# Exponent rows of a state-space layer: spread over partitions by one-hot matmuls, or by transfers from DRAM

## The chip, the cores and the metric

The kernel runs on one core of a Trainium2 chip. A core has TensorE for matmuls (PE in the profile, with its weight loads as PEld), VectorE (DVE), ScalarE (ACT), GpSimd (POOL) and SyncE (SP), each with a queue of its own that is worked off in order, and 16 DMA engines that all queues share. The metric is the time of one execution in device microseconds; the median of three runs before the change is 2631.59 us.

## The reference, cut to what matters

A two-layer encoder on 528 positions (16 meta tokens and 512 tokens) of 2048 channels, in float32. The change touches only the first layer's Mamba-2 branch, which has 32 heads in 8 groups of 4 and runs in both directions. The positions form 6 chunks of 88 in the kernel. For each head and direction, with `A_cs` the running sum of `log_a` inside a chunk:

```
seg    = A_cs[:, :, :, None] - A_cs[:, :, None, :]
Lmat   = exp(where(tri, seg, -inf))
CB     = einsum("bclgn,bcsgn->bclsg", Cc, Bc)
Y_diag = einsum("bclsgr,bcsgrp->bclgrp", CB[..., None] * Lmat, X)
Xd     = X * exp(A_cs[:, :, -1:] - A_cs)[..., None]
states = einsum("bclgn,bclgrp->bcgrpn", Bc, Xd)
...
Y_off  = einsum("bclgn,bcgrpn->bclgrp", Cc, prev) * exp(A_cs)[..., None]
y      = Y_diag + Y_off
```

Around it stand an input projection (97 weight panels of 128 columns, one of them half as wide), a 31-tap depthwise convolution on other channels, output projections, and a second layer with neighbourhood attention.

## The kernel before, in words

Channels lie on partitions and the 528 positions along the free axis. `proj` takes one panel of weights: two halves of 8 blocks, each weight split into a high and a low part (`wh` by ACT at L261, `wl` by DVE at L264), and for every block three products times two column halves of 264, so 96 matmuls into one PSUM tile `ps` (L308). There are two `ps` buffers, three of `raw` (the panel half as loaded by SP, L157), three of `wh` and of `wl`.

The layer's input projection runs over the groups `g` = 0 to 7. Each group takes one or two pairs of gated-convolution panels (`glu_tile`: gate `sg` L659 to L661, value `up` L666) and then six panels: `bT`, `cT`, two `xs` (each evacuated by DVE at L434 and convolved, L437 to L440) and two `zt` (evacuated by DVE at L685, SiLU at L686). After each panel `step()` lets two queues of background generators emit work up to a budget: `bgs` (budget `SB_` = 7000), which holds `ssd(g)`, and `bgc` (budget 6000), which holds `conv31` (31 taps on DVE, L452, ending in a store to `cv_d`, L455). `ssd(g)` is queued at the end of group g, so that it is emitted during the panels of group g+1. Each `yield` in it gives the budget that it has used; once a `step()` has used up its budget, the rest waits for the next panel.

`ssd(g)` does the following. It forms `pc`, the product of B and C (L555); for six chunks it transposes (L568), scales (L573) and multiplies out the states `st` (L578); then four steps of the recurrence over chunks on `pv` (L587, L590). Then come two halves `i` = 0, 1 of two heads `j` each. For each head it needs the row of running sums `fc` of that head, both directions, on every partition:

- `pf` = that row on all 128 partitions: two matmuls per direction with a one-hot column `sel` as stationary operand and `fhl` (the 64 rows of `fc` as a high and a low part) as moving one (L603);
- `T` (88 partitions): ReLU of `pf` against a column bias, chunk by chunk, 12 instructions of 88 by 88 on ACT (L606), Exp (L609), 12 scalings on ACT (L616), masks and sum on DVE (L617, L619);
- `cq` (128 partitions): Exp of `pf` on ACT (L608), times C on DVE (L610, L611).

With both heads done, 64 matmuls make `py` (L638); DVE adds and gates it (L642, L643), POOL stores it to `yz_d` (L644), and its square is added up using the `zt` tile as scratch (L648, L649). `T` and `cq` have two buffers each, so a half's tiles come free when the `py` of the half before is done. `pc`, `pf` and `py` share one PSUM buffer, the tag `big`. `zt` has two buffers: the two of the group being worked off by `ssd`, each free when its half is done.

The order of instructions on each engine is not the order of emission. A planner at build time (`schedule_with_timeline_sim=True`) simulates the program with its own costs and puts each engine's instructions into the order in which it sees them become ready, earlier emission first. On the chip that order is then fixed.

Of the kernel before, what the change touches and what calls it, by code (L numbers as in the profile page):

```python
# [12 lines left out]
F32 = mybir.dt.float32  # L13
F32R = mybir.dt.float32r
AF = mybir.ActivationFunctionType
ALU = mybir.AluOpType

P = 128
# [6 lines left out]
L = NM + S  # L25
HL = L // 2
# [4 lines left out]
HPG = 4  # L31
HD = 64
CH = 88
NC = L // CH
NH = 32
# [18 lines left out]
SB_, CB_ = 7000, 6000  # L54
# [29 lines left out]
def hybrid_encoder(ctx: ExitStack, tc: tile.TileContext, hT, win, wdt, wout, oin, oout, par, con,  # L84
                   rpb, out, dbg=None):
    nc = tc.nc
    dbg = dbg or {}

    cp = ctx.enter_context(tc.tile_pool(name="cp", bufs=1))
# [3 lines left out]
    dr = ctx.enter_context(tc.tile_pool(name="dr", bufs=1, space=bass.MemoryType.DRAM))  # L93
# [8 lines left out]
    def pool(**kw):  # L102
        return tc.tile_pool(reuse_waits="tile", **kw)

    def pr(n, a=0, b=None):
        lo, hi = PAR[n]
        return prm[:, lo + a:(hi if b is None else lo + b)]

    def cn(n):
        lo, hi = CON[n]  # L110
        return cst[:, lo:hi]
# [4 lines left out]
    def h2(ap):  # L116
        return ap.rearrange("p (a b) -> p a b", a=2)
# [2 lines left out]
        return h2(ap)[:, :, NB:]  # L120

    yz_d = dr.tile([KT, P, L], F32, name="yz_d")
    cv_d = dr.tile([KT, P, L], F32, name="cv_d")
    pt_d = dr.tile([KT, P, L], F32, name="pt_d")
    yb_d = dr.tile([KT, P, L], F32, name="yb_d")
# [29 lines left out]
    def load(a, hf, pool=None, tag="raw", bufs=3):  # L155
        raw = (pool or wp).tile([P, KH, a.shape[2]], F32, name=tag, tag=tag, bufs=bufs)
        nc.sync.dma_start(raw, a[:, hf * KH:(hf + 1) * KH, :])  # L157
        return raw
# [220 lines left out]
    with ExitStack() as c0:  # L379
        psb = c0.enter_context(tc.tile_pool(name="psb", bufs=1, space=bass.MemoryType.PSUM))  # L380
        sp = c0.enter_context(tc.tile_pool(name="sp", bufs=1))
        dp = c0.enter_context(tc.tile_pool(name="dp", bufs=1))
# [4 lines left out]
        nc.scalar.activation(rs0[:, 0:1], rs0[:, 0:1], AF.Sqrt)  # L387
        first_x = sp.tile([P, 2, L], F32, name="hraw", tag="T", bufs=2)
        wd0 = load(wdt, 0)
# [5 lines left out]
        fetch()()  # L395
        for tag, n, bufs in (("T", 2, 2), ("T", 2, 2), ("cq", 2, 2), ("cq", 2, 2), ("xb", 4, 1), ("pv", 4, 1)):
            t = first_x if not raws else sp.tile([P, n, L], F32, name="hraw", tag=tag, bufs=bufs)
            for i in range(n):
                k = len(raws)
# [17 lines left out]
                if k >= 2:  # L417
                    nc.vector.tensor_tensor(ac, ac, raw, op=ALU.add)

        sel = cp.tile([P, 64], F32R, name="sel")  # L420
        nc.vector.tensor_copy(sel, cn("sel"))
        xp = [sp.tile([P, L + 4], F32, name=f"xp{i}") for i in range(2)]
        for t in xp:
            nc.gpsimd.memset(t[:, 0:2], 0.0)
# [2 lines left out]
        J = 64  # L427
# [62 lines left out]

        t4 = [sp.tile([P, 2, L], F32, name=f"dt{i}", tag=tg, bufs=2) for i, tg in enumerate(("T", "T", "cq", "cq"))]
        v, e, w, z, la, fc, wd, dexp = [t4[i // 2][:J, i % 2] for i in range(8)]
# [25 lines left out]
        nc.gpsimd.memset(rf[:, ::CH], 0.0)  # L518
        nc.vector.tensor_tensor_scan(fc[0:32], rf[0:32], la[0:32], 0.0, ALU.mult, ALU.add)
        nc.vector.tensor_tensor_scan(fc[32:64, ::-1], rf[32:64], la[32:64, ::-1], 0.0, ALU.mult, ALU.add)  # L520
        fhl = dp.tile([P, L], F32R, name="fhl")
        nc.scalar.activation(fhl[:J], fc, AF.Copy)
        nc.vector.tensor_tensor(fhl[J:], fc, fhl[:J].bitcast(F32), op=ALU.subtract)
        fc3 = fc.rearrange("p (c t) -> p c t", c=NC)
        wd3 = wd.rearrange("p (c t) -> p c t", c=NC)
        nc.vector.tensor_tensor(wd3[0:32], fc3[0:32, :, CH - 1:CH].to_broadcast([32, NC, CH]), fc3[0:32], op=ALU.subtract)
# [14 lines left out]
        for nm, src in (("fcol", fc), ("dcol", dt), ("wcol", wd)):  # L541
# [3 lines left out]
            t = dp.tile([CH, NC, 2, NH], F32, name=nm)  # L545
            nc.vector.tensor_copy(t.rearrange("p c r h -> p (c r h)"), pt[:CH, :NC * J])
            cols.append(t)
        fcol, dcol, wcol = cols

        def ssd(g, bT, cT, xs, zs):  # L550
            xb = sp.tile([CH, NC, 3 * P], F32, name="xb", tag="xb")
            pv = sp.tile([P, NC - 1, 2, 256], F32, name="pv", tag="pv")
            pc = psb.tile([P, 2, 512], F32, name="pc", tag="big")
# [11 lines left out]
            for c in range(NC):  # L565
                pt = psb.tile([P, 512], F32, name="pt", tag="sm", bufs=2)
                for i, src in enumerate((xs[0], xs[1], bT)):
# [11 lines left out]
                                 start=True, stop=True)  # L579
# [12 lines left out]
            for i in range(2):  # L592
                gs, cs = [], []
                for j in range(2):
                    hl = 2 * i + j
                    hd = HPG * g + hl
                    T = sp.tile([CH, 2, L], F32, name="T", tag="T", bufs=2)
                    cq = sp.tile([P, 2, L], F32, name="cq", tag="cq", bufs=2)
                    for d in range(2):
                        pf = psb.tile([P, 2, 512], F32, name="pf", tag="big")  # L600
                        jj = d * NH + hd
                        for n in range(2):
                            nc.tensor.matmul(pf[:, n, :HL], sel[:, jj:jj + 1].to_broadcast([P, P]),  # L603
                                             fhl[:, n * HL:(n + 1) * HL], start=True, stop=True)
                        for c in range(NC):
                            nc.scalar.activation(T[:, d, c * CH:(c + 1) * CH], pf[:CH, c // 3, (c % 3) * CH:(c % 3 + 1) * CH],  # L606
                                                 AF.Relu, bias=fcol[:, c, d, hd:hd + 1], scale=-1.0)
                        nc.scalar.activation(h2(cq[:, d]), pf[:, :, :HL], AF.Exp)  # L608
                    nc.scalar.activation(T, T, AF.Exp, scale=-1.0)  # L609
                    nc.vector.tensor_tensor(cq[:, 0, CH:], cq[:, 0, CH:], cT[:, CH:], op=ALU.mult)  # L610
                    nc.vector.tensor_tensor(cq[:, 1, :L - CH], cq[:, 1, :L - CH], cT[:, :L - CH], op=ALU.mult)  # L611
                    yield 1050
                    for d in range(2):
                        for c in range(NC):
                            sl = slice(c * CH, (c + 1) * CH)
                            nc.scalar.activation(T[:, d, sl], T[:, d, sl], AF.Copy, scale=dcol[:, c, d, hd:hd + 1])  # L616
                        nc.vector.tensor_tensor(T[:, d], T[:, d], cbs[d], op=ALU.mult)  # L617
                    yield 1900
                    nc.vector.tensor_tensor(T[:, 0], T[:, 0], T[:, 1], op=ALU.add)  # L619
                    yield 650  # L620
                    gs.append(T)
                    cs.append(cq)
                py = psb.tile([P, 2, 512], F32, name="py", tag="big")
                for c in range(NC):
                    sl = slice(c * CH, (c + 1) * CH)
                    terms = [[], []]
                    for j in range(2):
                        hs = slice((2 * i + j) * HD, (2 * i + j + 1) * HD)
                        terms[j].append((xb[:, c, hs], gs[j][:, 0, sl]))
                        if c > 0:  # L630
                            terms[j].append((pv[:, c - 1, 0, hs], cs[j][:, 0, sl]))
                        if c < NC - 1:
                            terms[j].append((pv[:, NC - 2 - c, 1, hs], cs[j][:, 1, sl]))
                    nt = len(terms[0])
                    for q in range(nt):
                        for j in range(2):
                            a, b = terms[j][q]
                            nc.tensor.matmul(py[j * HD:(j + 1) * HD, c // 3, (c % 3) * CH:(c % 3 + 1) * CH], a, b,  # L638
                                             start=(q == 0), stop=(q == nt - 1))
                ti = 2 * g + i  # L640
                y = xs[i]
                nc.vector.scalar_tensor_tensor(h2(y), h2(y), pr("dd", ti, ti + 1), py[:, :, :HL], op0=ALU.mult, op1=ALU.add)  # L642
                nc.vector.tensor_tensor(y, y, zs[i], op=ALU.mult)  # L643
                nc.gpsimd.dma_start(yz_d[ti], y)  # L644
                if ti == 0:
                    nc.scalar.activation(accy, y, AF.Square)
                else:
                    nc.scalar.activation(zs[i], y, AF.Square)  # L648
                    nc.vector.tensor_tensor(accy, accy, zs[i], op=ALU.add)  # L649
                yield 2100  # L650

        def step():
            pump(bgs, SB_)
            pump(bgc, CB_)
# [56 lines left out]
    with ExitStack() as c1:  # L711
        psb = c1.enter_context(pool(name="psc", bufs=1, space=bass.MemoryType.PSUM))
        zb = c1.enter_context(pool(name="zbp", bufs=14))
        big = c1.enter_context(pool(name="big", bufs=16))
# [33 lines left out]
        for m in range(KT):  # L748
            ps = proj(us, ls)
            t = zb.tile([P, L], F32, name="zb", tag="zb")  # L750
# [301 lines left out]
    with ExitStack() as c2:  # L1052
        psb = c2.enter_context(pool(name="psd", bufs=1, space=bass.MemoryType.PSUM))
        ak = c2.enter_context(pool(name="ak", bufs=1))
        ap = c2.enter_context(pool(name="ap", bufs=1))
# [181 lines left out]
        with tc.manual_schedule(engines={eng.PE, eng.DVE, eng.Activation, eng.Pool}):  # L1237
# [6 lines left out]
            g = filler()  # L1244
# [72 lines left out]
    with ExitStack() as c3:  # L1317
        psr = c3.enter_context(pool(name="pr", bufs=1, space=bass.MemoryType.PSUM))
        op = c3.enter_context(pool(name="op", bufs=NRES))
# [60 lines left out]
        for m in range(2 * NORMF):  # L1380
# [7 lines left out]
            t = op.tile([P, S], F32, name="fo", tag="o")  # L1388
# [221 lines left out]
```

## Time and profile before

| | |
|---|---|
| median of the runs | 2631.59 us (2630.65 to 2633.07) |
| profiled execution: time, span | 2635.39 us, 2633.6 us |
| granted TensorE clock | 0.996 |
| PE, PEld, DVE, ACT, POOL busy over the span | 99%, 94%, 78%, 54%, 14% |
| first matmul `pf` to last | 148.9 to 1046.0 us |
| `pf` matmuls (L603) | 128 |
| Exp of `pf` into `cq` (L608) | 64, 40.0 us in all |
| GpSimd's DMA queue | 78.30 MB, 11.1% of the 16 engines |

The span is divided among the first layer's input projection, which holds everything that the change touches and ends at about 1290 us, and later stages that it leaves alone. A line of the profile gives a line of the kernel, the engine, the operation, output and inputs by name, and times; "x6" means six instructions; what follows "<-" is what released a wait. The profiled execution's time is 3.8 us above the median of the runs.

### The profile page before, as it was taken

What the parts mean: (1) busy time and instruction counts of PE and PEld (TensorE: products, weight loads), DVE (VectorE), ACT (ScalarE), POOL (GpSimd) and SP (SyncE); (2) the same over time, 40 slices, a digit from 0 to 9 for tenths busy, and PEclk for the clock granted to TensorE, in tenths of its full rate; (3) what the DMA queues carried; (4) which work ended last, traced back from release to release, by engine and by line L of the source; (5) the groups of instructions that cost most, each with busy time, mean ns of one, the idle gap of its engine ahead of it and who ended that gap; (6) DMA issues with size and microseconds to landing.
All of it is one profiled execution on the core that took longest, in us unless ns stands there. A gap on an engine that the chain in (4) does not pass through costs nothing.

```text
span 2633.6 us, 52716 instructions
## 1 busy us (share of the span) xinstructions
PE 2599.0 (99%) x21236; PEld 2484.8 (94%) x21236; DVE 2051.0 (78%) x3046; ACT 1419.4 (54%) x2652; POOL 367.5 (14%) x588
## 2 busy tenths in 40 slices
PE   8999999999999999999999999999999999999997
PEld 8999999999999999999999999999999987777797
DVE  6985967887686969997688888877777776666876
ACT  5366585666658566325554556644334355556543
POOL 0000000000000001100220312300000052442133
PEclk9999999999999999999999999999999999999998
DMA  4322223222222222533875877755555454543754
GB/s 173 99 75 93 81 77 97 82 94 74 92 85 76 88 90 92 177 109 111 268 232 166 297 216 236 238 159 163 154 152 159 142 155 124 134 128 116 244 171 152
DMA packets 163173, 373.28 MB, mean 142 GB/s; under 512 B 40896, under 2 KB 70784, under 8 KB 162928
## 3 DMA queue, kind: packets, MB, share of 16 engines
q1 hardware_dynamic: 137840, 289.96, 34.5%
q0 software_dynamic: 23072, 78.30, 11.1%
q8 instruction: 167, 2.74, 0.4%
q10 hardware_dynamic: 2016, 1.65, 0.2%
q14 instruction: 78, 0.64, 0.1%
HBM read 320.59 MB, written 49.25 MB: 140 GB/s over the span
## 4 chain that ended last, share of the span: by engine, by line
PE 88%; DVE 4%; ACT 3%; DMA 3%; issue 1%; SPq 0%; POOL 0%; DVEq 0%; ACTq 0%; POOLq 0%
PE ps L308 44%; PE pb L285 28%; PE ps L1190 6%; PE py L638 2%; PE po L1176 2%; DVE wl L264 1%; PE st L578 1%; PE pq L1127 1%; DVE a L452 1%; ACT T L606 1%; ACT L608 1%; ACT wh L261 1%; PE pa L1151 1%; DMA srf<-o_d 1%; PE pf L603 0%
## 5 line engine op out<-in xcount | busy, mean ns | idle before, releaser
L308 PE MATMUL ps<-rh,wh 128*128 128x264 f32 (+2 forms) x3520 | 730.7, 287 | 9.6 <-ACT rh L325 8.5
L308 PE MATMUL ps<-rh,wl 128*128 128x264 f32 (+2 forms) x3520 | 730.3, 287 | 0.0
L308 PE MATMUL ps<-rl,wh 128*128 128x264 f32 (+2 forms) x3520 | 725.9, 287 | 0.6 <-DVE rl L326 0.5
L261 ACT ACTIVATE wh<-raw 128x1024 fp32r<-128x1024 f32 (+1 forms) x349 | 369.0, 1057 | 531.2 <-PE ps L308 272.7
L308 PEld LDWEIGHTS ps<-rh,wh 128*128 128x128 f32 (+1 forms) x3520 | 549.3, 189 | 15.7 <-ACT rh L325 9.1
L264 DVE TENSOR_TENSOR wl<-raw,wh 128x1024 fp32r<-128x1024 f32 (+1 forms) x349 | 439.8, 1260 | 159.1 <-ACT wh L261 154.4
L308 PEld LDWEIGHTS ps<-rh,wl 128*128 128x128 f32 (+1 forms) x3520 | 548.9, 188 | 2.0
L308 PEld LDWEIGHTS ps<-rl,wh 128*128 128x128 f32 (+1 forms) x3520 | 546.7, 188 | 4.1 <-DVE rl L326 1.5
L285 PE MATMUL pb<-rh,wh 128*128 128x264 f32 (+1 forms) x1280 | 364.6, 285 | 1.8 <-ACT wh L261 1.0
L285 PE MATMUL pb<-rl,wh 128*128 128x264 f32 (+1 forms) x1280 | 363.4, 284 | 0.0
L285 PE MATMUL pb<-rh,wl 128*128 128x264 f32 (+1 forms) x1280 | 362.6, 284 | 0.0
L452 DVE SCALAR_TENSOR_TENSOR a<-up,prm,a 128x528 f32<-128x528 f32 x464 | 343.2, 770 | 2.3 <-ACT a L447 0.9
L285 PEld LDWEIGHTS pb<-rh,wh 128*128 128x128 f32 x1280 | 242.4, 189 | 3.0 <-DVE fo L1474 1.5
L285 PEld LDWEIGHTS pb<-rl,wh 128*128 128x128 f32 x1280 | 242.1, 189 | 0.0
L285 PEld LDWEIGHTS pb<-rh,wl 128*128 128x128 f32 x1280 | 241.5, 189 | 0.0
L285 PE MATMUL pb<-ta,wh 128*128 128x264 f32 (+1 forms) x1280 | 235.3, 283 | 0.4 <-ACT wh L261 0.4
L285 PEld LDWEIGHTS pb<-ta,wh 128*128 128x128 f32 x1280 | 197.9, 189 | 0.7 <-ACT wh L261 0.6
L261 ACT ACTIVATE wh<-wy 128x1024 fp32r<-128x1024 f32 x109 | 115.5, 1060 | 136.9 <-PE pb L285 98.6
L285 PE MATMUL pb<-ta,wl 128*128 128x264 f32 (+1 forms) x640 | 181.9, 285 | 3.4 <-DVE wl L264 3.3
L264 DVE TENSOR_TENSOR wl<-wy,wh 128x1024 fp32r<-128x1024 f32 x109 | 140.2, 1287 | 55.7 <-ACT wh L261 55.7
L261 ACT ACTIVATE wh<-wb 128x1024 fp32r<-128x1024 f32 x80 | 84.7, 1059 | 101.4 <-PE pb L285 61.6
L285 PEld LDWEIGHTS pb<-ta,wl 128*128 128x128 f32 x640 | 120.4, 188 | 4.4 <-DVE wl L264 4.4
(389 smaller groups left out, 4123.9 us busy)
## 6 DMA issues: line engine op xcount, KB each, us to landing
raw<-win SPq DMA_DIRECT2D x192, 512.0 KB, 3.6
raw<-oin SPq DMA_DIRECT2D x84, 512.0 KB, 4.4
raw<-wout SPq DMA_DIRECT2D x40, 512.0 KB, 5.2
wb<-oin SPq DMA_DIRECT2D x22, 512.0 KB, 3.9
wy<-oin SPq DMA_DIRECT2D x22, 512.0 KB, 3.7
wy<-oin POOLq DMA_DIRECT2D x22, 512.0 KB, 8.0
raw<-oout SPq DMA_DIRECT2D x20, 512.0 KB, 4.8
srt<-h_d POOLq DMA_DIRECT2D x38, 264.0 KB, 5.4
```

What stands on the lines that cost most here:

```text
L261: nc.scalar.activation(wh, raw, AF.Copy)
L264: nc.vector.tensor_tensor(wl, raw, wh.bitcast(F32), op=ALU.subtract)
L285: nc.tensor.matmul(acc, w[:, k, :], u[:, lo + o:lo + o + n], start=(new and k == 0 and j == 0), stop=(k == KH - 1 and j == 2), skip_group_ ...
L308: nc.tensor.matmul(ps[:M, n, :N], w[:, k, :], u[:, lo + n * HL:lo + n * HL + N], start=(kk == 0 and j == 0), stop=(kk == KT - 1 and j == 2))
L452: nc.vector.scalar_tensor_tensor(a, u[:, j:j + L], wv(j), a, op0=ALU.mult, op1=ALU.add)
L578: nc.tensor.matmul(st[:, :nd * 256], xb[:, c, 256:], xd[:, d0:d1].rearrange("p r x -> p (r x)"), start=True, stop=True)
L606: nc.scalar.activation(T[:, d, c * CH:(c + 1) * CH], pf[:CH, c // 3, (c % 3) * CH:(c % 3 + 1) * CH], AF.Relu, bias=fcol[:, c, d, hd:hd + 1 ...
L608: nc.scalar.activation(h2(cq[:, d]), pf[:, :, :HL], AF.Exp)
L638: nc.tensor.matmul(py[j * HD:(j + 1) * HD, c // 3, (c % 3) * CH:(c % 3 + 1) * CH], a, b, start=(q == 0), stop=(q == nt - 1))
L1127: nc.tensor.matmul(pqs[a, w][:, :n], x[hs, w * P:(w + 1) * P], y[hs, st:st + n], start=(j == 0), stop=(j == 2))
L1176: nc.tensor.matmul(self.po[hs, w * P:(w + 1) * P], lt, rt, start=(q == 0), stop=(q == nq - 1))
L1190: nc.tensor.matmul(h2(ps) if lo is None else ps, w[:, k, :], tok(u) if lo is None else u[:, lo:lo + S], start=(kk == 0 and j == 0), stop=( ...
```

## The change

The one-hot matmuls go. The 64 rows of `fc`, and their exponentials, are computed once (`ef`, one Exp on ACT) and stored into a DRAM tile `f_d` by two transfers of GpSimd. A helper `rows(g, i)` then loads, for each of the two heads of a half, `T` as the raw row repeated on 88 partitions and `cq` as the exponential repeated on 128 partitions, each with both directions, by one transfer of GpSimd each whose source has a step of zero over the partitions. ACT's ReLU works on `T` in place, and the Exp into `cq` is gone. The loads of the first half are issued at the head of `ssd(g)`, those of the second half right behind the first half's `py`. After the first half `ssd` yields twice more with the full budget, so that the second half is emitted two panels later than its loads.

```diff
+    f_d = dr.tile([2, 2 * NH, L], F32, name="f_d")
...
-        sel = cp.tile([P, 64], F32R, name="sel")
-        nc.vector.tensor_copy(sel, cn("sel"))
...
-        fhl = dp.tile([P, L], F32R, name="fhl")
-        nc.scalar.activation(fhl[:J], fc, AF.Copy)
-        nc.vector.tensor_tensor(fhl[J:], fc, fhl[:J].bitcast(F32), op=ALU.subtract)
+        nc.gpsimd.dma_start(f_d[0], fc)
+        ef = e
+        nc.scalar.activation(ef, fc, AF.Exp)
+        nc.gpsimd.dma_start(f_d[1], ef)
...
+        def rows(g, i):
+            out = []
+            for j in range(2):
+                hd = HPG * g + 2 * i + j
+                T = sp.tile([CH, 2, L], F32, name="T", tag="T", bufs=2)
+                cq = sp.tile([P, 2, L], F32, name="cq", tag="cq", bufs=2)
+                for k, t in enumerate((T, cq)):
+                    s = f_d[k, hd]
+                    nc.gpsimd.dma_start(t, bass.AP(tensor=s.tensor, offset=s.offset,
+                                                   ap=[[0, t.shape[0]], [NH * L, 2], [1, L]]))
+                out.append((T, cq))
+            return out
+
         def ssd(g, bT, cT, xs, zs):
+            rw = rows(g, 0)
...
-                    T = sp.tile([CH, 2, L], F32, name="T", tag="T", bufs=2)
-                    cq = sp.tile([P, 2, L], F32, name="cq", tag="cq", bufs=2)
+                    T, cq = rw[j]
                     for d in range(2):
-                        pf = psb.tile([P, 2, 512], F32, name="pf", tag="big")
-                        jj = d * NH + hd
-                        for n in range(2):
-                            nc.tensor.matmul(pf[:, n, :HL], sel[:, jj:jj + 1].to_broadcast([P, P]),
-                                             fhl[:, n * HL:(n + 1) * HL], start=True, stop=True)
                         for c in range(NC):
-                            nc.scalar.activation(T[:, d, c * CH:(c + 1) * CH], pf[:CH, c // 3, (c % 3) * CH:(c % 3 + 1) * CH],
-                                                 AF.Relu, bias=fcol[:, c, d, hd:hd + 1], scale=-1.0)
-                        nc.scalar.activation(h2(cq[:, d]), pf[:, :, :HL], AF.Exp)
+                            sl = slice(c * CH, (c + 1) * CH)
+                            nc.scalar.activation(T[:, d, sl], T[:, d, sl], AF.Relu, bias=fcol[:, c, d, hd:hd + 1], scale=-1.0)
...
+                if i == 0:
+                    rw = rows(g, 1)
                 ti = 2 * g + i
...
                 yield 2100
+                if i == 0:
+                    yield SB_
+                    yield SB_
```

## The prediction

> **What bounds the kernel now.** I read the page first, then the busy time by stretches, the groups by line, the chain of waits through one group, and last the engines in order of time. First TensorE, over the span and over the stretch that holds the change, with columns PE, PEld, DVE, ACT, POOL, clock, DMA share and GB/s:
>
> ```profile
> PE 2599.0 (99%) x21236; PEld 2484.8 (94%) x21236; DVE 2051.0 (78%) x3046; ACT 1419.4 (54%) x2652; POOL 367.5 (14%) x588
> ```
> ```profile
> 100.00:1160.00 1060.00, 1057.80 (x9104) 1025.72 (x9103) 846.40 (x1155) 632.96 (x1359) 55.54 (x88) 1.00 0.28 93
> ```
>
> In 1060 us PE stands still for 2.2 us. A matmul taken out of its queue should therefore shorten the run by what it occupies, if nothing else becomes late. What the change touches, by line:
>
> ```profile
> L261 ACT ACTIVATE wh<-raw 128x1024 fp32r<-128x1024 f32 x158 | 168.1, 1064 | 275.0 <-PE ps L308 183.6 <-issue 90.9
> L616 ACT ACTIVATE T<-T,dcol 88x88 f32<-88x88 f32 x384 | 103.4, 372 | 0.5
> L606 ACT ACTIVATE T<-pf,fcol 88x88 f32<-88x88 f32 x384 | 91.8, 336 | 19.8 <-PE pf L603 19.7
> ...
> L608 ACT ACTIVATE cq<-pf 128x528 f32<-128x528 f32 x64 | 40.0, 624 | 0.3
> L609 ACT ACTIVATE T<-T 88x1056 f32<-88x1056 f32 x32 | 35.2, 1101 | 0.0
> ...
> L608 ACT ACT_TABLE_LOAD x26 | 33.4, 1283 | 0.2
> ...
> L638 PE MATMUL py<-T,xb 88*64 88x88 f32 x384 | 41.8, 244 | 0.6 <-ACT cq L608 0.6
> ...
> L603 PE MATMUL pf<-fhl,sel 128*128 128x264 f32 x128 | 27.1, 292 | 1.4 <-ACT cq L608 1.4
> ...
> L603 PEld LDWEIGHTS pf<-fhl,sel 128*128 128x128 f32 x128 | 19.6, 188 | 2.2 <-ACT cq L608 2.2
> ```
>
> The 27.1 us of L603 are not its price, since a matmul starts before the one ahead of it has ended. The chain of waits shows the real cadence (start, length, what). Below are the group's start, `pc` at 363.42, then its second half, and the next group's `pc` at 473.89, 110.5 us later:
>
> ```profile
> 363.42 0.94 PE pc L555 x12
> ...
> 433.16 2.45 PE py L638 x60
> 435.61 3.49 PE ps L308 x27
> 439.10 0.26 PE pf L603 x2
> ...
> 448.94 0.52 PE pf L603 x2
> 449.45 7.29 PE ps L308 x60
> 456.74 0.24 PE pf L603 x2
> ...
> 467.80 2.60 PE py L638 x62
> ...
> 473.89 0.94 PE pc L555 x12
> ```
>
> 60 matmuls of 264 columns take 7.29 us, 0.1215 us each, and a pair of `pf` 0.24 us. The chain passes through ACT before 448.94, but PE works on panels meanwhile: all that it stands before L603, over eight groups, is the 1.4 us of the group row above.
>
> **The change, part by part.**
>
> *Matmuls.* Removed are 128 x 0.1215 = 15.6 us of PE. Their covers are gone too: the 1.4 us that PE stood before L603 for ACT. Together -17.0 us; if PEld's own waits there (at most another 2.2 us of the idle shown) count in full, -19.2.
>
> *ACT.* The 64 Exps of `cq` go, 40.0 us; one of 64 rows comes instead (about 0.6, from the 624 ns). The ReLUs now read the tile in SBUF as L616 does. Rows in order of time:
>
> ```profile
> 439.38 1.44 ACT L606 ACTIVATE T<-pf,fcol 88x88 f32<-88x88 f32 x6 [1.53 <-PE pf L603]
> ...
> 449.88 3.22 ACT L616 ACTIVATE T<-T,dcol 88x88 f32<-88x88 f32 x12
> ```
>
> Six take 1.44 us (0.24 each), twelve from SBUF 3.22 us (0.27): 384 x 0.03 = 11 us more. The 26 table loads of L608 move to L609, which has 32 instructions, so at most 6 more, 8 us. ACT gains some 20 us in all. It is 60% busy in the stretch, so that counts at nothing except inside a half, where it forms the chain.
>
> *DVE.* It loses two small instructions before the first group: nothing.
>
> *POOL and its queue.* 64 loads and 2 stores are added. The nearest row for a transfer with two pieces per partition, and for a plain one:
>
> ```profile
> 1669.86 0.72 POOL L774 DMA_DIRECT2D accy<-vqk_d  x1 [5.14 <-PE ps L308]
> ```
> ```profile
> 437.46 0.55 POOL L644 DMA_DIRECT2D yz_d<-cv  x1 [21.12 <-DVE cv L643]
> 466.18 1.32 POOL L661 TENSOR_TENSOR sg<-sg,rs 128x528 f32<-128x528 f32 x1 [28.17 <-ACT sg L660]
> ```
>
> 66 x 0.72 = 48 us on an engine that is 55.5 us busy in 1060. What matters is order: each load waits for the `py` that frees its tile, and behind it on POOL stand `yz_d` and `sg`. The four loads of a second half wait until 435.6 and hold POOL for 2.9 us; `yz_d` goes out at 438.5 instead of 437.5, and nobody waits for it then. `sg` is 28 us away. I put POOL at nothing.
>
> *Transfers.* `T` of one head is 88 x 2 rows of 2112 bytes, 363 KB; `cq` 128 x 2, 528 KB; a half 1782 KB, 16 halves 29.2 MB, or 31 GB/s over the 930 us of the eight groups, beside the 93 shown. Nothing before reads one DRAM row on many partitions; the nearest is `bt`, whose rows overlap in DRAM. For a burst on POOL's queue I take the one at 1067 us, where twelve loads go out together (issues: size, median us to landing):
>
> ```profile
> xc<-cv_d POOLq DMA_DIRECT2D x12, 264.0 KB, 7.1
> raw<-win SPq DMA_DIRECT2D x3, 512.0 KB, 6.6
> ```
> ```profile
> tq<-vqk_d POOLq DMA_DIRECT2D x1, 256.0 KB, 3.1
> bt<-rpb SPq DMA_DIRECT2D x30, 132.5 KB, 3.6
> ```
>
> So the first `T` of a half lands 3.1 us (a lone load of 256 KB) to 7.1 us after its issue; I take 4.5, nearer to the lone one because it is first in its burst. Scaling `bt` by size gives 363/132.5 x 3.6 = 9.9, the bad end. SP's panel loads suffer at most as in that burst, 6.6 us instead of 3.6; with three `raw` buffers a load may go out once the half three before it is split, so at least one panel, 96 x 0.1215 = 11.7 us, lies between issue and use. Nothing.
>
> Halves differ in their cover. The rows of DVE through the same group:
>
> ```profile
> 398.49 0.70 DVE L619 TENSOR_TENSOR T<-T 88x528 f32<-88x528 f32 x1
> ...
> 418.94 0.70 DVE L460 TENSOR_TENSOR accl<-accl,a 128x528 f32<-128x528 f32 x1
> ...
> 428.49 0.68 DVE L590 TENSOR_TENSOR pv<-pv,rt 128x512 f32<-128x512 f32 x1
> ...
> 463.95 0.70 DVE L619 TENSOR_TENSOR T<-T 88x528 f32<-88x528 f32 x1
> ...
> 470.44 0.76 DVE L642 SCALAR_TENSOR_TENSOR cv<-cv,prm,py 128x528 f32<-128x528 f32 x1 [4.64 <-PE py L638]
> ...
> 473.94 0.71 DVE L685 TENSOR_TENSOR zt<-ps,rs 128x528 f32<-128x528 f32 x1
> ...
> 478.78 0.71 DVE L666 TENSOR_TENSOR up<-ps,sg 128x528 f32<-128x528 f32 x1 [0.75 <-PE ps L308]
> ...
> 483.51 2.81 DVE L452 SCALAR_TENSOR_TENSOR a<-up,prm,a 128x528 f32<-128x528 f32 x4
> ```
>
> *The first half* has 30 us of cover: its last `T` is ready at 399, and its `py` waits for the recurrence on `pv`, which ends at 429. *The second half* has none, since its loads can only start when the first `py` is done.
>
> Before: from the end of `py` at 435.6 to the last `T` at 464.65, 29.0 us. After: issue 0.7, landing 4.5 (440.8); twelve ReLUs 3.2, table 1.28, Exp 1.1, scalings 3.2; the second head 3.2 + 1.1 + 3.2; three `wh` splits of 1.05; DVE 1.4: 461.7. At 7.1 us for the landing it is 464.3. So the chain is 3 us shorter to no longer. The two added yields only lower the second half's rank by two panels; DVE's `conv31` work, which could now rank ahead of it, lies elsewhere (its last instruction at 419, the next at 484), so I cost them at nothing.
>
> What costs is that PE takes `py` at a fixed place in its queue. `T` is complete at 464.65 and `py` starts at 467.80: 3.15 us of margin. If the chip is later than the planned order by more than that, PE stands, in each group. Before, the pair at 448.94 held PE until ACT had caught up; now the lateness adds up from 435.6. How late loads on POOL come against their place in the order is seen where ACT meets one:
>
> ```profile
> ACT rh L806 <- DMA sr<-t_d: 14.5, 12, 2.6
> ```
>
> 12 waits of 1.2 us on average, 2.6 at most. With one table load of 1.28 us that may not be in the plan, lateness is 1.2 + 1.28 = 2.5 (no stall) to 2.6 + 1.28 = 3.9 (0.7 us). I take 0.4 us, about the middle, and 8 groups: +3.2 us. The ends: 0, and 7.1 - 3.1 = 4.0 plus 1.28 less 3.15 = 2.1 us, +17.
>
> *The sum:* -15.6 - 1.4 + 3.2 = -13.8 us. The profiled execution has 2635.4 us around a span of 2633.6; its time would be 2621.6. It lies 3.8 above the median 2631.6, so the forecast in the runs is 2631.6 - 13.8 = 2617.8.
>
> A rule to weigh here. The rows show a lone 256 KB in 3.1 us on POOL's queue, on 128 partitions. The Trainium skill, page "DMA: Bandwidth & Descriptors", section "Why a DMA increments its semaphore by 16 and not by 1", says that a transfer uses the largest number of engines up to 16 that divides the slowest dimension on both sides; 88 rows would get 11 of 16, though it adds that some transfers issued by software on trn2 were seen to keep 16. By that rule, as an estimate, `T` would move at 11/16 of the rate and land about 0.6 us later, which makes the sum 8 x 0.6 = 5 us worse, 2622.6; no row of before has a transfer of 88 partitions.
>
> **The rivals.**
>
> *Even: the wait moves to `py`.* The first `T` lands at the burst's 7.1 us, and the margin is gone: 2.1 us x 8 = 17 against 17.0. For it: no cover in the second half. Against: the burst's 7.1 is the median of twelve loads, and this one is the first of four. 2631.6.
>
> *Slower: the broadcast row is slow to read.* If many partitions reading one DRAM row lands like `bt`, the first `T` takes 9.9 us, 6.8 more than the lone load: 6.8 + 1.28 - 3.15 = 4.9 us of standing PE per group, 8 x 4.9 = 39. The same lateness reaches `zt`: its PSUM tile is read at 473.94 only because the second half is done, and PE needs that tile at 478.8, so 4 us of delay is all that is free there. 2631.6 - 17.0 + 39 = 2654. It turns slower from 17/8 = 2.1 us of stall per group. Against it: `bt` has a fixed part that I scaled along, so 9.9 is too high.
>
> *DVE holds the end.* From 975 us on it has hardly a gap:
>
> ```profile
> 975.00:1184.00 209.00, 208.75 (x1777) 206.31 (x1777) 200.50 (x269) 91.59 (x168) 24.76 (x34) 1.00 0.38 122
> ```
>
> There the last group's savings (16 `pf`, 1.95 us) could be lost, and if that stretch didn't move forward at all, the whole 13.8. But its work comes with the panels, which move forward with PE, and PE is at 208.75 of 209: inside the forecast's range, 2 us at most.
>
> **How the numbers follow.** Forecast 70% (2612 to 2626; stalls of 0 to 1.4 us per group), even 15%, slower 15%. A measurement of this kernel tells about 0.2%, 5.3 us: faster is below 2626.3. The range runs from 2631.6 - 19.2 = 2612 to the even case, 2632, and leaves out the slower rival and a little below.
>
> **What would show it.** L603 and the Exps of L608 gone; PE's busy time in the stretch down by some 16 us; 64 loads of 363 and 528 KB on POOL's queue, the `T` landing in 4 to 6 us; idle time before L638 ended by `T`, up from 0.6 us to 3 or so; period of a group 108.5 to 109 us instead of 110.5. The prediction is wrong if PE's idle time before L638 or before `ps` exceeds 17 us, if L606 waits on the transfer for more than 8 us per group, or if panels wait for `zt`.

## The result, and the profile after

| | before | after |
|---|---|---|
| median of the runs, same chip | 2632.33 us (2630.65 to 2633.48) | 2664.01 us (2663.59 to 2669.80) |
| profiled execution: time, span | 2635.39, 2633.6 us | 2664.13, 2662.4 us |
| granted TensorE clock | 0.996 | 0.989 |

The change makes the kernel slower by a ratio of 1.0128 [1.0116, 1.0140], about 32 us, where the prediction had 14 us less. A row of the page of after, and the stretch of 1060 us that holds the change (columns PE, PEld, DVE, ACT, POOL, clock, DMA share, GB/s):

```profile
PE 2595.4 (97%) x21108; PEld 2480.4 (93%) x21108; DVE 2051.4 (77%) x3044; ACT 1391.8 (52%) x2580; POOL 416.5 (16%) x654
```
```profile
100.00:1160.00 1060.00, 1024.13 (x8712) 991.94 (x8711) 824.90 (x1122) 597.23 (x1277) 102.20 (x152) 0.98 0.37 117
```

The 128 matmuls are gone, yet PE stands 35.9 us of these 1060, not 2.2, and its clock there is 0.98. The two pages give a balance. The span grew by 28.8 us. PE's idle time grew from 34.6 to 67.0, 32.4 us more. Its busy time fell by 3.6; if the removed work is the 15.6 of the prediction, the matmuls that are left take 12.0 us longer. 32.4 + 12.0 - 15.6 = 28.8.

Where PE stands, and who waits for the new transfers (us in total, times, longest):

```profile
PE st L592 <- DVE xd L587: 23.5, 9, 4.3
PE py L645 <- ACT T L623: 8.8, 3, 3.1
...
PE py L645 <- DVE T L626: 2.6, 1, 2.6
```
```profile
ACT T L615 <- DMA T<-f_d: 44.8, 15, 4.7
```
```profile
DVE cq L617 <- DMA cq<-f_d: 64.1, 27, 8.1
```

The largest loss is at the states `st`, which use neither `T` nor `cq`. One such place in order of time, first POOL and ACT, then DVE, then PE (start, length, idle time before it and its releaser):

```profile
239.97 1.51 POOL L558 DMA_DIRECT2D T<-f_d  x2 [29.55 <-PE py L645]
```
```profile
245.25 5.04 ACT L615 ACTIVATE T<-T,fcol 88x88 f32<-88x88 f32 x19 [2.35 <-DMA T<-f_d]
250.29 1.28 ACT L698 ACT_TABLE_LOAD   x1
...
254.24 1.28 ACT L672 ACT_TABLE_LOAD   x1
...
256.19 1.28 ACT L616 ACT_TABLE_LOAD   x1
257.49 1.08 ACT L616 ACTIVATE T<-T 88x1056 f32<-88x1056 f32 x1
258.48 0.47 ACT L583 ACTIVATE xb<-pt 88x384 f32<-88x384 f32 x1
```
```profile
258.98 0.42 DVE L587 TENSOR_TENSOR xd<-xb,wcol 88x256 f32<-88x256 f32 x1 [4.28 <-ACT xb L583]
```
```profile
246.71 0.49 PE L582 MATMUL pt<-cst,cv 128*88 128x128 f32 x3
...
259.45 1.22 PE L592 MATMUL st<-xd,xb 88*128 88x256 f32 x2 [3.24 <-DVE xd L587]
```

PE had the transposed chunk `pt` ready at 247.2. ACT copies it to `xb` only at 258.48, because 23 ReLUs of a first half stand ahead of it in its queue; they waited 2.35 us for `T`, which can be loaded only once the `py` of the half before has freed the tile. Three table loads (3.84 us) also stand ahead of `xb`. `xd` on DVE comes at 258.98, and PE, in order too, stands 3.24 us. The other places are alike: ahead of each of the seven stands of more than 1 us before `st`, ACT had waited 1.8 to 4.7 us for `T` within the last 30 us. The plan itself had changed: in the trace of before 0, 0, 6, 12, 24 and 24 ReLUs of this group's first half stand ahead of its six `xb`, in after 23 and then 24 each time.

A place in a second half, where `py` itself is late:

```profile
332.01 6.33 ACT L615 ACTIVATE T<-T,fcol 88x88 f32<-88x88 f32 x24 [3.10 <-DMA T<-f_d]
...
339.30 1.28 ACT L616 ACT_TABLE_LOAD   x1
340.60 1.09 ACT L616 ACTIVATE T<-T 88x1056 f32<-88x1056 f32 x1
341.70 1.28 ACT L698 ACT_TABLE_LOAD   x1
343.00 0.65 ACT L698 ACTIVATE zt<-zt 128x528 f32<-128x528 f32 x1
343.66 1.28 ACT L616 ACT_TABLE_LOAD   x1
```
```profile
351.72 0.53 PE L645 MATMUL py<-T,xb 88*64 88x88 f32 x2 [3.09 <-ACT T L623]
```

A SiLU of `zt` stands between the two Exps, so three table loads lie in the chain where the prediction counted one.

### The profile page after: what moved, and what is told of

It is laid out like the page before. It is cut to its first block, busy times and chain, and to the rows that moved or that the text cites. A ratio compares the mean times of both kernels' runs of the same rounds, so it can differ in the third digit from the quotient of the medians.

```text
span 2662.4 us, 52485 instructions
## 1 busy us (share of the span) xinstructions
PE 2595.4 (97%) x21108; PEld 2480.4 (93%) x21108; DVE 2051.4 (77%) x3044; ACT 1391.8 (52%) x2580; POOL 416.5 (16%) x654
## 4 chain that ended last, share of the span: by engine, by line
PE 74%; ACT 8%; DVE 6%; issue 6%; DMA 5%; POOL 1%; SPq 0%; DVEq 0%; POOLq 0%; ACTq 0%
PE ps L309 33%; PE pb L286 28%; PE ps L1202 6%; ACT T L615 2%; DMA T<-f_d 2%; ACT wh L262 1%; DVE wl L265 1%; PE py L645 1%; ACT T L623 1%; PE st L592 1%; PE po L1188 1%; DVE a L451 1%; DMA cq<-f_d 1%; PE pq L1139 1%; ACT L616 1%
## 5 line engine op out<-in xcount | busy, mean ns | idle before, releaser
L309 PEld LDWEIGHTS ps<-rh,wh 128*128 128x128 f32 (+1 forms) x3520 | 553.0, 190 | 13.7 <-ACT rh L326 8.2
L262 ACT ACTIVATE wh<-wy 128x1024 fp32r<-128x1024 f32 x109 | 115.5, 1060 | 135.1 <-PE pb L286 97.3
L615 ACT ACTIVATE T<-T,fcol 88x88 f32<-88x88 f32 x384 | 102.9, 354 | 47.0 <-DMA T<-f_d 44.8
```

Source lines behind the costliest of these rows:

```text
L262: nc.scalar.activation(wh, raw, AF.Copy)
L309: nc.tensor.matmul(ps[:M, n, :N], w[:, k, :], u[:, lo + n * HL:lo + n * HL + N], start=(kk == 0 and j == 0), stop=(kk == KT - 1 and j == 2))
L615: nc.scalar.activation(T[:, d, sl], T[:, d, sl], AF.Relu, bias=fcol[:, c, d, hd:hd + 1], scale=-1.0)
```

## The experiments

The theory (A) after this reading: the loads are hidden or not by where the planned order puts their users on ACT and DVE. The rivals: the loads as such (their bytes, their queue, the repeated row), the second half as forecast, or the yields. In all that follow, "before" is the kernel before on the same chip.

**No loads.** The four transfers of a half are left out; the ReLU reads an old tile `rs0` instead of `T`, the product reads it instead of `cq`, so the kernel leaves out the rows that both need.

```diff
-                for k, t in enumerate((T, cq)):
-                    s = f_d[k, hd]
-                    nc.gpsimd.dma_start(t, ...)
...
-                            nc.scalar.activation(T[:, d, sl], T[:, d, sl], AF.Relu, ...)
+                            nc.scalar.activation(T[:, d, sl], rs0[:CH, sl], AF.Relu, ...)
...
-                    nc.vector.tensor_tensor(cq[:, 0, CH:], cq[:, 0, CH:], cT[:, CH:], op=ALU.mult)
+                    nc.vector.tensor_tensor(cq[:, 0, CH:], rs0[:, CH:], cT[:, CH:], op=ALU.mult)
```

> The 64 loads are left out: ReLU and the product with C take a fixed tile (rs0) as input, so the values are wrong, and every instruction on PE, ACT and DVE stays. Theory A (the loss is lateness of the loaded tiles against an order of instructions fixed in advance): PE no longer stands before st (23.5 us) or py (11.4 us), the granted clock goes back to 0.996, time 2613 to 2618 us, the 17 us gain of the prediction. Rival C (it is the new order itself, without pf and with the second half emitted two panels later, that is bad, whatever the loads do): 2635 us or more. An even result near 2632 would mean that the matmuls taken out bring nothing.

2621.32 us against 2631.32, ratio 0.9961 [0.9945, 0.9976]; a little above what A expected. Waits of PE, then ACT at the same place:

```profile
PE st L588 <- DVE xd L583: 3.9, 4, 1.0
PE py L641 <- DVE T L622: 2.9, 4, 0.7
```
```profile
230.82 6.33 ACT L611 ACTIVATE T<-rs,fcol 88x88 f32<-88x88 f32 x24 [2.95 <-issue]
...
248.45 0.47 ACT L579 ACTIVATE xb<-pt 88x384 f32<-88x384 f32 x1
```

So without the loads the change gains some 10 us. The planner made a new order for this kernel, but in it, too, all 24 ReLUs of a first half stand ahead of the `xb` of every chunk, in every group. That order costs little as long as nobody waits in it: PE stands 3.9 us before `st`, not 23.5.

**One half alone.** The other half keeps its matmuls (`i == 0` or `i == 1` through `pf` as before) and has no loads.

```diff
-                    T, cq = rw[j]
+                    if i == 0:   # the half that keeps pf; 1 in the other kernel
+                        ... pf by matmuls, ReLU and Exp from it ...
+                    else:
+                        T, cq = rw[j]
```

> First half of each group again by one-hot matmuls, second half by transfers; 64 of 128 pf matmuls are gone (7.8 us). Theory A (the first half's loads come late for ACT and DVE, which then hold up the evacuation of xb and xd that PE waits for at st; some 23.5 us of standing PE plus a slow clock after it): st waits vanish, py waits of 3 us in some groups stay, 2634 to 2644 us. Rival (the prediction's own view: the first half is covered, only the second is exposed): the loss stays, 2655 us or more.

> First half by transfers, second half again by one-hot matmuls; 64 of 128 pf matmuls are gone (7.8 us). Theory A: waits before st stay at some 20 to 25 us and the clock drops after them, py waits vanish, 2645 to 2660 us. Rival (only the second half is exposed): 2622 to 2628 us.

Second half only: 2626.35 us, ratio 0.9981 [0.9971, 0.9991], better than A expected. First half only: 2659.21 us, ratio 1.0102 [1.0086, 1.0118], a time as A expected, though the waits before `py`, which A had vanish, are 5.9 us. PE's waits, of the second half's kernel and then of the first half's:

```profile
PE py L665 <- DVE T L646: 4.5, 3, 2.2
```
```profile
PE st L597 <- DVE xd L592: 17.1, 12, 4.5
PE py L665 <- DVE T L646: 5.9, 4, 2.5
```

The half that the prediction gave 30 us of cover is the one that costs; the half without cover loses little. The two effects (-5 and +28 us) don't add up to +32, so each plan has its own stalls.

**The repeated row.** The loads read distinct rows of another DRAM tensor, with the same shapes and bytes; the kernel leaves out the rows of `f_d`. The order on PE, ACT and DVE stays that of after.

```diff
-                    s = f_d[k, hd]
+                    s = hT[hd % 8 + k]
...
-                                                   ap=[[0, t.shape[0]], [NH * L, 2], [1, L]]))
+                                                   ap=[[L, t.shape[0]], [P * L, 2], [1, L]]))
```

> Loads of the same size and shape, but every partition reads a DRAM row of its own (from the input hT) instead of all reading one row; the values are wrong, the instructions the same. Theory A (it is the order, and the landing time is that of any such burst): T lands in about 6.6 us and cq in 8.6 us as before, 2664 us within 5. Rival B (the prediction's slower rival: one DRAM row read by many partitions is slow): T lands in 3 to 5 us and the time falls by 20 us or more.

2667.89 us, ratio 1.0137 [1.0124, 1.0151]: no gain. The issues of after, and of this kernel (size, median us to landing):

```profile
cq<-f_d POOLq DMA_DIRECT2D x32, 528.0 KB, 8.6
...
T<-f_d POOLq DMA_DIRECT2D x32, 363.0 KB, 6.6
```
```profile
cq<-hT POOLq DMA_DIRECT2D x32, 528.0 KB, 8.2
T<-hT POOLq DMA_DIRECT2D x32, 363.0 KB, 6.4
```

A row read by many partitions lands like distinct rows, within 0.4 us.

**SyncE's queue instead of GpSimd's.**

```diff
-                    nc.gpsimd.dma_start(t, ...)
+                    nc.sync.dma_start(t, ...)
```

> The 64 loads issued by SP instead of GpSimd. Theory A: SP issues them faster and they land a few us sooner, T in 4 to 5 us instead of 6.6, so waits before st and py shrink by a third, 2645 to 2660 us; but SP's queue then waits for py ahead of panel loads, which could cost as much. Rival B (landing is bound by bandwidth, not by the queue): the landing times stay, 2664 us or more.

2694.03 us, ratio 1.0242 [1.0225, 1.0259]: far from A's range, and 30 us above the least that B gave. Both waits of PE grow:

```profile
PE st L592 <- DVE xd L587: 31.2, 10, 5.1
PE py L645 <- DVE T L626: 17.6, 8, 4.7
```

With 2.9 us more for ACT that is 20.5 us before `py` (11.4 in after), and ACT's wait for `T` rises from 44.8 to 65.6 us. SP's queue also carries the panels; that its order is what delays the loads was not separated. The planned order is another one, and the trace has no landing times for SP's loads, so neither A's faster landing nor B's equal one is shown. Taking the loads off GpSimd brought nothing.

**No yields.**

```diff
-                if i == 0:
-                    yield SB_
-                    yield SB_
```

> The change without the two added yields, so that the second half is emitted right after the first. The prediction costs them at nothing: 2664 us within 5. If they serve to cover the loads of the second half, py waits grow (11.4 us now) and the time rises by 10 us or more; if they hurt, it falls.

2666.94 us, ratio 1.0129 [1.0115, 1.0144], with `st` at 21.5 us: no difference to the change with them. The traces show why: every engine works off the same instructions in the same order in both kernels. The planner gave the same plan with and without the yields, so they did nothing, and the 2.9 us between the two medians is what two measurements of one plan differ by.

**ReLUs behind chunk 1.** One engine's order is changed: on ACT the ReLUs of a group may not stand ahead of the `xb` of its chunk 1.

```diff
+                xi = nc.scalar.activation(xb[:, c, :], ...)
+                if c == 1:
+                    xlast = xi.ins
...
+                            with tc.issue_after(xlast):
                                 nc.scalar.activation(T[:, d, sl], T[:, d, sl], AF.Relu, ...)
```

> Transfers as in the change; the only edit pins the ReLUs of both halves behind the evacuation of the second chunk's xb in ACT's queue (issue order, no wait). Theory A (in ACT's queue the ReLUs, waiting for their load, stand ahead of xb): st waits of the first chunks fall from 23.5 us to under 8, 2630 to 2648 us. Rival B (the transfers as such are too slow or take bandwidth from the panels): no change, 2664 us.

2665.88 us, ratio 1.0128 [1.0112, 1.0144]: a miss, nothing gained. PE's stand before `st` falls from 23.5 to 12.7 us, but 13.7 us before `ps` and `pt` are new (0.8 in after). DVE and PE at the same place in this kernel:

```profile
256.42 0.62 DVE L620 TENSOR_TENSOR cq<-cq,cv 128x440 f32<-128x440 f32 x1 [7.42 <-DMA cq<-f_d]
257.48 0.68 DVE L589 TENSOR_TENSOR xd<-xb,wcol 88x512 f32<-88x512 f32 x1
```
```profile
258.22 2.08 PE L594 MATMUL st<-xd,xb 88*128 88x512 f32 x2 [5.80 <-DVE xd L589]
```

Now DVE stands 7.42 us for `cq`, with `xd` behind it; its `xb` was written at 250. So the theory was incomplete: DVE's queue can hold the states too.

**Both queues, and each alone.** ReLUs behind the `xb` of the last chunk on ACT, products of `cq` and C behind the `xd` of the last chunk on DVE; then each of the two alone.

```diff
+                if c == 5:
+                    xlast, dlast = xi.ins, xj.ins     # xj: the xd of this chunk
...
+                            with tc.issue_after(xlast):
                                 nc.scalar.activation(T[:, d, sl], T[:, d, sl], AF.Relu, ...)
...
+                    with tc.issue_after(dlast):
                         nc.vector.tensor_tensor(cq[:, 0, CH:], cq[:, 0, CH:], cT[:, CH:], op=ALU.mult)
```

> The change, with the ReLUs pinned behind the evacuation of the last chunk's xb in ACT's queue and the products of cq with C pinned behind the last chunk's xd in DVE's queue (issue order, no wait); all transfers stay as they are. Pinning ACT's queue alone left 12.7 us of PE standing before st, with DVE held 7.4 us by a load of cq that stood ahead of xd. Theory A, widened to both queues: nothing of the first half can hold up the states any more, st waits under 3 us, clock 0.996, 2618 to 2628 us. Rival B (the transfers themselves slow the panels): stays above 2645 us.

> Only DVE's order is changed: the products of cq and C stand behind the xd of the last chunk; ACT keeps the ReLUs of the first half ahead of some xb. Theory A (an in-order queue of either engine is enough to hold the states, since xd needs xb and xb stands behind the waiting ReLUs): PE still stands before the states, 10 to 20 us in all, and the time is 2642 to 2665 us. Rival (DVE's queue alone is what delays the states, and ACT has time to catch up): waits before the states under 5 us, 2615 to 2630.

> Only ACT's order is changed: the ReLUs stand behind the xb of the last chunk (the earlier one-engine run had them behind chunk 1); DVE keeps the products ahead of some xd. Theory A: as in that run, PE stands before the states for DVE, 10 to 20 us, 2645 to 2668 us. Rival (that run missed only because the ReLUs still stood ahead of chunks 2 to 5): waits before the states under 5 us, 2615 to 2630.

| order pinned on | median us | ratio to before | PE stands before `st`, us | before `py`, us | before `ps`, us |
|---|---|---|---|---|---|
| neither (after) | 2664.01 | 1.0128 [1.0116, 1.0140] | 23.5 | 11.4 | 0.8 |
| DVE | 2680.63 | 1.0188 [1.0172, 1.0203] | 21.6 | 12.2 | 7.6 |
| ACT | 2652.08 | 1.0078 [1.0065, 1.0091] | 1.9 | 19.7 | 4.1 |
| both | 2619.09 | 0.9956 [0.9941, 0.9970] | 0 | 3.4 | 1.7 |

DVE alone, then ACT alone, then the stretch and the waits with both:

```profile
PE st L594 <- DVE xd L587: 21.6, 9, 3.7
PE py L648 <- ACT T L626: 8.3, 2, 4.6
...
PE py L648 <- DVE T L629: 3.9, 3, 1.9
```
```profile
PE py L648 <- ACT T L626: 19.4, 5, 5.2
...
PE st L594 <- DVE xd L587: 1.9, 1, 1.9
```
```profile
100.00:1160.00 1060.00, 1054.86 (x9082) 1024.38 (x9081) 857.19 (x1171) 605.57 (x1289) 101.73 (x154) 1.00 0.39 122
```
```profile
PE py L649 <- DVE T L630: 3.4, 3, 1.9
```

With both pinned PE stands 5.1 us in the stretch and the clock is back at 1.00, with the same transfers: `T` lands after a median of 6.3 us, `cq` 8.4 (6.6 and 8.6 in after), and ACT and DVE still wait for them, 25.9 and 37.2 us. Those waits no longer hold PE, because nothing that PE needs soon stands behind them. This version came out as A expected and beats the kernel before by 12.5 us, although the execution that the profile shows took 6.7 us more than the median.

DVE alone came out as A expected at `st`, and slower than A's bound. ACT alone came in at A's time, but not at A's place: at `st` only 1.9 us are left, and 19.7 us stand before `py`. Pinning re-plans the rest as well. With ACT alone the SiLU of `zt` stands between the two Exps in five of the eight second halves, and it is at the `py` of these five that PE stands the 19.4 us; in after it is so in three second halves, and PE stands at the `py` of these three and of one more; with both pinned, and in before, it is so in none. So of the 45 us between after and both, the part at `st` is shown to come from the order, nearly all of it from ACT's. The part at `py` goes with the place of the SiLU, which no run changed by itself; why pinning DVE too moves it is open.

**Both queues, no yields; both queues, one load per head.** The second has one load of the raw row on 128 partitions, the ReLU reads it there, and the Exp of `cq` is back on ACT.

```diff
+                s = f_d[0, hd]
+                nc.gpsimd.dma_start(cq, bass.AP(..., ap=[[0, P], [NH * L, 2], [1, L]]))
...
+                                nc.scalar.activation(T[:, d, sl], cq[:CH, d, sl], AF.Relu, ...)
+                    nc.scalar.activation(cq, cq, AF.Exp)
```

> Both orders pinned, without the two added yields. Theory A: the yields only lower the rank of the second half in the planned order and bring nothing: within 0.3% of the two-pin version, 2613 to 2627. Rival (with the first half's stalls gone, the two panels of distance are what covers the second half's loads): py waits of 2 to 3 us per group, 16 to 24 us more, 2633 to 2645.

> Both orders pinned, and one load per head instead of two: the raw row on 128 partitions into cq, the ReLU reads it there, and the Exp of cq is back on ACT in place (32 of 128 by 1056, about 1.2 us each, 38 us on ACT). Theory A: half as many loads, 1056 instead of 1782 KB per half, so the first row lands 1 to 2 us earlier (median 5 to 6 us instead of 6.3), but ACT has 2.4 us more inside each half; with both the second half comes no earlier, and the time is that of the two-pin version within 0.3%, 2613 to 2627. Rival (the size of the burst is what still costs): under 2612. Rival (ACT inside a half is what costs): 2628 to 2640.

Without yields: 2619.87 us, ratio 0.9956 [0.9942, 0.9970], the same as with them, and again the same order on every engine. One load: 2637.47 us, ratio 1.0023 [1.0014, 1.0032], the last rival's range. Its issues and waits:

```profile
cq<-f_d POOLq DMA_DIRECT2D x32, 528.0 KB, 6.1
```
```profile
PE py L645 <- DVE T L626: 6.5, 5, 2.2
```

1056 KB per half instead of 1782 bring the median landing that the ReLU waits for only from 6.3 to 6.1 us, and ACT's busy time in the stretch rises from 605.6 to 626.4. But PE also stands 8.5 us before `ps`, for panels' splits and a `sg` that come late (1.7 with two loads), more than the 7.9 before `py`. So that ACT inside a half is what costs is not shown; ACT's longer queue may delay the panels as well.

Loading earlier, with a third buffer for `T` and `cq`, wasn't tried.

## Why the prediction was wrong

*The step that failed* is "the first half has 30 us of cover", costed at nothing. It asked when `T` and `cq` are needed (by `py`, late) and not what stands behind their users. For POOL the prediction did go through the queue behind the waiting instruction; for ACT and DVE it did not. It read the cover off the order of before, where the ReLUs stand among the `xb`; the new plan put them ahead. The recurrence that was to cover the wait is fed by `xb` and `xd`, which stand in those two queues behind it. The first half alone costs 28 us where 0 was written, and 17.1 us of PE's standing there are before `st`. The Trainium skill, page "PSUM — Partial Sum Buffer", section "Engine vs sequencer instructions", says that the queues of ScalarE, VectorE and GpSimd are strictly first in, first out; the rows at 245.25 and 258.48 agree.

*Matmuls*, -17.0: right in kind. Without loads it is -10.0 us by the medians, with loads in a better order -12.2 and -12.5, each with waits still in it. The whole sum, -13.8, is about what the version with both queues pinned reaches: the forecast describes a plan that the kernel didn't have.

*The first landing*: from the `py` to the first ReLU 5.2 us were worked out (0.7 + 4.5); the rows at 239.97 and 245.25 give 5.28. Right. The medians over both heads of a half, 6.6 for `T` and 8.6 for `cq`, are higher.

*The second half's stall*, 0.4 us per group, 3.2 in all, end 17: measured 11.4 in after, 4.5 in the kernel with that half alone. Right in kind, too small in after. One term was mis-sized: one table load was counted in the new chain, where the place shown has three, and the trace of before has three in the chain that was compared with it:

```profile
440.82 1.28 ACT L608 ACT_TABLE_LOAD   x1
...
442.75 1.28 ACT L686 ACT_TABLE_LOAD   x1
...
446.98 1.28 ACT L608 ACT_TABLE_LOAD   x1
```

The two left out are 2.6 us, most of the margin of 3.15.

*POOL, SP's panel loads, DVE, the yields, all at nothing*: POOL is busy 416.5 us instead of 367.5, 49 more where 48 were counted, and no group of PE's waits names it; `raw` lands in 3.7 us (3.6 before); the yields made no difference in two pairs of kernels, since the planned order is the same with and without them; the second half did not rank lower.

*The rivals*: the slower one gave 2654 through a repeated row that lands late and `zt` behind it; distinct rows land the same, so its mechanism fell though its sign was right. Its turning point, 2.1 us of stall per group, was passed, but at `st`. "DVE holds the end" was not tested by itself.

*The rule on 88 rows* was not tested by itself, and its 0.6 us was given without a working. That 363 KB on 88 partitions land after a median of 6.3 us (both queues pinned) and 528 KB on 128 after 6.1 (one load per head) goes its way, but the bursts differ (four loads and two).

*What would show it*: PE's idle time before `py` stayed under 17 us, and ACT's wait for `T` at 5.6 us per group under 8. The watch list had no entry for `st`; by its marks of being wrong the change would have looked harmless. Two of its other marks did miss: `T` lands in 6.6 us, not 4 to 6, and a group takes 112 us or more, not 108.5 to 109.

## What to carry to other kernels

When a transfer takes the place of work on an engine, look at its first user on each in-order engine and list what stands behind it there; cover counts only if nothing on the way to the bottleneck is in that list. If an order is fixed at build time, a load that lands later than the plan has it can be harmless in one order and cost 45 us in another, so pin the feeders of the bottleneck ahead of the users of the load, on every engine that has both. Pin all of them: one of the two alone gave 12 us or took 17, both gave 45. And compare the order of the engines in the two traces before reading a difference as the effect of an edit: the yields left the plan as it was, and leaving the loads out made another plan.

## What the runs showed of the hardware

A short stand of PE costs more than its length. A place in after where PE stood, and the 4 us that follow five such places (PE busy, matmuls, clock, DMA share, GB/s):

```profile
708.05 0.34 PE L645 MATMUL py<-T,xb 88*64 88x88 f32 x2 [2.83 <-ACT T L623]
```
```profile
230.87:234.87 4.00, 4.00 (x22) 0.66 0.40 124
259.45:263.45 4.00, 4.00 (x18) 0.58 0.23 60
...
622.19:626.19 4.00, 4.00 (x31) 1.00 0.02 4
708.05:712.05 4.00, 4.00 (x38) 1.00 0.00 0
736.02:740.02 4.00, 4.00 (x16) 0.50 0.14 54
```

Of eleven stands of 1.68 to 4.28 us in the stretch, nine were followed by a clock of 0.50 to 0.66 over the next 4 us; the one of 1.68 and one of 2.83 were not, while the one of 2.60 that ended at 230.87 was. Windows of 4 us blur this: the trace has the clock at 0.50 nine times in the stretch, six times for 3.41 us (first from 232.11 to 235.52) and three times for 6.83 (first from 733.87 to 740.70). PE was busy for 36.1 of these 40.9 us, so about 18 us were lost, 1.6 us and more each time. The 12.0 of the balance is less, but it rests on the estimate of 15.6: in the version with both queues pinned and no yields PE's busy time fell by 20.4 us for the same matmuls, and with that the balance gives 16.8.

The Trainium skill, page "TensorE: Matmul & The Clock Gate", Part 1, says that the clock halves after at least one idle window of about 3.4 us, and that the window runs freely, so that the moment of a change depends on where in the window the work falls. The trace agrees in part: nearly equal stands end differently, and the half clock starts at whole multiples of 3.41 us (232.11, 259.42 and 351.58 lie 8 and 27 of them apart); but 2.60 us of standing was enough here, and 1.93 us was enough in the version with both queues pinned (the stand that ended at 902.85). No run here gives the threshold. The prediction priced stalls at their length alone.
